# The last four k tiles of the last 512 output features computed token-major in three token groups, in a hybrid decoder step on one core

## The chip, the core and the metric

The kernel runs on one core of a Trainium2 chip. The number that counts is the device time of one execution in microseconds. Before the change it is 1300.18 us, the median of three runs (1300.1 to 1300.28). The engines are named as in the profile: PE multiplies matrices, DVE, ACT and POOL work on tiles, SP issues DMAs. [...] Each engine works through its own queue in order and waits there for what an instruction needs from others.

## What is computed

One layer of a hybrid decoder over 264 tokens (256 of a prompt and 8 samples) and 2048 features. Mixers, gates and projections come first. The change lies in the last two lines of this cut:

```python
def rms_norm(x, g):
    y = x * lax.rsqrt(jnp.mean(x * x, axis=-1, keepdims=True) + EPS)
    return y * g
...
    x = x + (g_a * y_pool + g_b * y_lru + g_c * y_conf) @ w_out
    hid = jnp.square(jax.nn.relu(rms_norm(x, g_mlp) @ w_up))     # 2048 -> 8192
    x = x + hid @ w_down                                         # 8192 -> 2048
...
    y = rms_norm(x, g_final)
```

## The kernel before

**Layout.** Everything is feature-major: a tile has 128 features on the partitions and the 264 tokens (`N`) along the row. The residual `X` is 16 such tiles (`KD`). A product takes a 128x128 piece of a weight matrix as its stationary operand and streams the 264 tokens past it, so a PSUM bank collects one output tile of 128 features by 264 tokens.

**Precision.** Weights arrive as fp32 in `raw`, six slots of 128x1024 filled by DMAs from SP (`dma_pair`, L134). For each such chunk ACT rounds the weights to `whi` (L163) and DVE forms the remainder `wlo` (L164). Activations are kept as such pairs as well; for the last quarter of the MLP they are `LH` and `Q`. Each product is therefore three matmuls (`mm3`, L186 to L188): high by high, high weight by low activation, low weight by high activation.

**Order.** `weight_plan` lists groups of weights; a group is a set of k tiles against 512 output features (four PSUM banks), a chunk is two k tiles of it. The main loop goes through the chunks: it splits the chunk three ahead, sends for the one eight ahead, multiplies the present one, and at the end of a group evacuates the four banks. The MLP is done in four quarters `q`; each quarter computes 2048 hidden features and then multiplies them by 2048 rows of `w_down` in four groups `m` of 512 output features. The very last two chunks are taken together, one output tile after the other, so that the four banks of the last group become complete one at a time.

**The end.** In quarter 3, `down_evac` (L826) adds each finished bank to `X` on DVE. ACT squares the tile into `G` (`square_add`, L795), POOL adds the square to a running sum `sq2` (L798), and ACT scales `X` by the final gain (L837). After the last tile, six matmuls with `ones` (L982) sum the squares over the partitions and spread the sum over all 128 partitions, in two halves of 132 tokens. ACT takes the inverse root (L988), DVE refines it by a Newton step (L994 to L998), and DVE and POOL multiply the 16 tiles of `X` by this factor in pieces (L1003), each piece sent to `y_dram` by a DMA from SP or ACT (L1005). All code after the loop is written out by hand in the order in which each engine gets it.

Of the kernel before, what the change touches and what calls it, by code (L numbers as in the profile page):

```python
# [13 lines left out]
ALU = mybir.AluOpType  # L14
# [7 lines left out]
KD = D // P  # L22
EPS = 1e-6
LN_EXP = "natural_log_exp_and_others"
ROOT = "abs_reciprocal_sqrt_and_small"
# [5 lines left out]
           ("b_lru_x", 8), ("lru_lambda", 8), ("w_conf_conv", 124), ("b_conf_conv", 4), ("g_conf", 4),  # L31
           ("b_conf", 4), ("b_gate", 48), ("g_mlp", 16), ("g_final", 16), ("count", 16)]
PCOL, _at = {}, 0
# [19 lines left out]
SINGLE = 4  # L53
WIDE = 4
ROW = N + CH


def weight_plan():

    groups = [("w_lru_in", 0, 2 * WIDE, 0)] + [("w_in", WIDE, KD - WIDE, m) for m in (1, 2)]
    groups += [("w_in", 0, 16, m) for m in (0, 3, 4, 6, 5)]
    for g in range(4):
        groups += [("w_gate", 0, 16, t) for t in ((0, 4, 1), (5,), (2, 6), (3, 7))[g]]
        groups += [("w_pool_br", 0, 4, g), ("w_lru_br", 0, 8, g)]
    groups += [("w_gate", 0, 16, 8 + g) for g in range(3)]
    groups += [("w_conf_br", 0, 4, 0), ("w_gate", 0, 16, 11)]
    groups += [("w_conf_br", 0, 4, g) for g in range(1, 4)]
    groups += [("w_out", 0, 16, m) for m in range(4)]  # L70
    for q in range(4):
        groups += [("w_up", 0, 16, q * 4 + m) for m in range(4)]
        groups += [("w_down", q * 16, 16, m) for m in range(4)]
    chunks = []
    for gi, (name, _, k, m) in enumerate(groups):
        for c in range(k // 2):
            chunks.append(("wide" if name == "w_lru_in" else "dense", gi, c, CH))
            if name == "w_in" and (m, c) in LRU_AT:
                chunks.append(("lru", LRU_AT.index((m, c)), 0, 512))
            if (name, m) == ("w_gate", 0) and c == 3:  # L80
                chunks += [("grp", 0, 0, 512), ("none", 0, 0, 0)]
    return groups, chunks


@with_exitstack
def hybrid_step(ctx: ExitStack, tc: tile.TileContext, head_in, x_in, par_in, st_in, wall, y_out, st_out):
    nc = tc.nc
# [27 lines left out]
    sp = cpool.tile([P, 16], F32, name="sp")  # L115
    gfin = cpool.tile([P, KD], F32, name="gfin")

# [705 lines left out]
    def half(h):  # L823
        return slice(h * (N // 2), (h + 1) * (N // 2))

    def down_evac(q, m, ps):  # L826
        if (q, m) == (3, KD - 1):
            for h in range(2):
                nc.vector.tensor_tensor(X[:, m, half(h)], X[:, m, half(h)], res(ps)[:, h, :], op=ALU.add)
                nc.vector.tensor_tensor(G[:, 11, half(h)], X[:, m, half(h)], X[:, m, half(h)], op=ALU.mult)  # L830
            return
        nc.vector.tensor_tensor(halves(X[:, m, :]), halves(X[:, m, :]), res(ps), op=ALU.add)  # L832
        spend(dve=0.4)
        if q == 3:
            def rest():
                square_add(m, m < KD - 2)
                nc.scalar.activation(X[:, m, :], X[:, m, :], AF.Copy, scale=gfin[:, m:m + 1])  # L837

            later(0 if m >= KD - 4 else 1 + m % 4 // 2, rest)

# [77 lines left out]
    for i, ch in enumerate(chunks):  # L918
# [18 lines left out]
        if kind == "dense":  # L937
            rhs, fn = group(gi)
            n = groups[gi][2] // 2
            if c == 0:  # L940
                pss = [acc() for _ in range(4)] if gi > 2 else pair[4 * gi - 4:4 * gi]
            if i < len(chunks) - 2:
                for kt in range(2):
                    if i == 13 and kt == 1:
                        x_rms()
                    for m in range(4):
                        tile_mm(i, gi, c, kt, m, rhs, pss, c == n - 1 and kt == 1)
            elif i == len(chunks) - 1:
                for m in range(4):
                    for b in range(4):  # L950
                        tile_mm(i - 1 + b // 2, gi, c - 1 + b // 2, b % 2, m, rhs, pss, b == 3)
            if c == n - 1:
                for m in range(4):
                    fn(m, pss[m])
                after(gi)
        elif kind == "lru":
            for j in range(2):
                lru_gate_mm(2 * gi + j, i, j)
            if gi == 3:
                lru_tail()  # L960
        elif kind == "grp":
            grp_mm(i)
        if i == len(chunks) - 4:
            nc.scalar.preload_act_table_set(ROOT)
        if i == 140:
            nc.sync.dma_start(st_out, st)
        if 5 <= i < 9:
            x_squares(i - 5)
# [9 lines left out]

    ps = [acc(), acc()]
    for k, t in enumerate((20, 21 + (KD - 2) % 3, 11)):  # L980
        for h in range(2):
            nc.tensor.matmul(ps[h][:, half(h)], ones, G[:, t, half(h)], start=k == 0, stop=k == 2)  # L982
    Y = raw.rearrange("p a c -> p (a c)")[:, :KD * N].rearrange("p (h k n) -> p h k n", h=2, k=KD)
    t, last = G[:, 9, :], acc()
    factor, seed2 = G[:, 10, :], G[:, 12, half(1)]

    for h in range(2):
        nc.scalar.activation(rstd[:, half(h)], ps[h][:, half(h)], AF.Abs_reciprocal_sqrt, bias=eps)  # L988
    nc.scalar.activation(X[:, KD - 1, :], X[:, KD - 1, :], AF.Copy, scale=gfin[:, KD - 1:KD])

    def newton(h):
        c = half(h)
        if h:
            nc.vector.scalar_tensor_tensor(t[:, c], ps[h][:, c], EPS, seed2, op0=ALU.add, op1=ALU.mult)  # L994
        else:
            nc.vector.scalar_tensor_tensor(t[:, c], ps[h][:, c], EPS, rstd[:, c], op0=ALU.add, op1=ALU.mult)
            nc.vector.tensor_tensor(t[:, c], t[:, c], rstd[:, c], op=ALU.mult)
        nc.vector.scalar_tensor_tensor(factor[:, c], t[:, c], -3.0, rstd[:, c], op0=ALU.add, op1=ALU.mult)  # L998
        nc.scalar.copy(last[:, c], factor[:, c])

    def scaled(eng, queue, h, a, b, by):
        k = slice(a, b)
        eng.tensor_tensor(Y[:, h, k, :], X[:, k, half(h)], by[:, None, half(h)].to_broadcast([P, b - a, N // 2]),  # L1003
                          op=ALU.mult)
        queue.dma_start(y_out[:, h, k, :], Y[:, h, k, :])  # L1005

    def own(h, a, b):
        scaled(nc.gpsimd, nc.scalar, h, a, b, factor)

    def wide(h, a, b, by=last):  # L1010
        scaled(nc.vector, nc.sync, h, a, b, by)

    newton(0)
    nc.scalar.activation(seed2, rstd[:, half(1)], AF.Square)
    wide(0, 0, 2, factor)
    own(0, 11, 13)
    wide(0, 2, 5)
    wide(0, 5, 8)
    own(0, 13, 16)
    wide(0, 8, 11)  # L1020
    newton(1)
    wide(1, 0, 4, factor)
    own(1, 11, 16)
    wide(1, 4, 11)

# [91 lines left out]
```

## Time and profile before

| | us |
|---|---|
| median of three runs (lowest, highest) | 1300.18 (1300.1, 1300.28) |
| the profiled execution | 1299.8 |
| its span, from first to last instruction | 1298.0 |
| PE busy | 1287.7 |
| DVE busy | 833.2 |
| ACT busy | 718.4 |
| POOL busy | 113.6 |
| mean DMA rate | 198 GB/s |

The profile is one execution. Its span is 1.8 us shorter than that execution's own time, and the execution is 0.4 us faster than the median of the runs. A row of a timeline shows start, duration, engine, line, operation and tiles. `PEld` is the loading of a stationary operand, `SPq` and `ACTq` are the queues that issue DMAs. A mean duration in a group of instructions is that of one instruction, which can be longer than the distance between two, since instructions overlap on an engine.

### The profile page before, as it was taken

What the parts mean: (1) busy time and instruction counts of PE and PEld (TensorE: products, weight loads), DVE (VectorE), ACT (ScalarE), POOL (GpSimd) and SP (SyncE); (2) the same over time, 40 slices, a digit from 0 to 9 for tenths busy, and PEclk for the clock granted to TensorE, in tenths of its full rate; (3) what the DMA queues carried; (4) which work ended last, traced back from release to release, by engine and by line L of the source; (5) the groups of instructions that cost most, each with busy time, mean ns of one, the idle gap of its engine ahead of it and who ended that gap; (6) DMA issues with size and microseconds to landing.
All of it is one profiled execution on the core that took longest, in us unless ns stands there. A gap on an engine that the chain in (4) does not pass through costs nothing.

```text
span 1298.0 us, 26711 instructions
## 1 busy us (share of the span) xinstructions
PE 1287.7 (99%) x11434; PEld 1286.8 (99%) x11434; DVE 833.2 (64%) x1056; ACT 718.4 (55%) x1024; POOL 113.6 (9%) x149
## 2 busy tenths in 40 slices
PE   9999999999999999999999999999999999999997
PEld 9999999999999999999999999999999999999996
DVE  6886898776776677666655455655555655565554
ACT  7767677667674655455544334543344533354544
POOL 0250010110102023131000000000000000000113
PEclk9999999999999999999999999999999999999998
DMA  9655556555565564655555555555555555555561
GB/s 348 214 185 199 196 202 205 194 195 195 199 228 193 185 208 157 233 187 203 196 198 194 196 197 195 195 198 195 196 196 196 194 197 195 196 196 197 196 202 68
DMA packets 39287, 256.96 MB, mean 198 GB/s; under 512 B 4352, under 2 KB 5504, under 8 KB 10240
## 3 DMA queue, kind: packets, MB, share of 16 engines
q1 hardware_dynamic: 38736, 254.58, 57.7%
q8 instruction: 89, 1.46, 0.4%
q10 hardware_dynamic: 432, 0.68, 0.1%
q14 instruction: 30, 0.25, 0.1%
HBM read 252.03 MB, written 3.21 MB: 197 GB/s over the span
## 4 chain that ended last, share of the span: by engine, by line
PE 99%; issue 0%; POOLq 0%; POOL 0%; DVE 0%; ACT 0%; ACTq 0%
PE acc L188 33%; PE acc L186 33%; PE acc L187 33%; PE acc L896 1%; PE acc L302 0%; POOLq L1096 0%; POOL raw L1003 0%; POOL G L798 0%; PE acc L260 0%; DVE X L832 0%; ACT G L795 0%; POOLq L1003 0%; POOLq L798 0%; ACTq L795 0%
## 5 line engine op out<-in xcount | busy, mean ns | idle before, releaser
L164 DVE TENSOR_TENSOR wlo<-raw,whi 128x1024 fp32r<-128x1024 f32 (+1 forms) x479 | 586.4, 1226 | 442.6 <-ACT whi L163 436.8
L163 ACT CAST whi<-raw 128x1024 fp32r<-128x1024 f32 (+1 forms) x479 | 493.4, 1033 | 525.7 <-PE acc L187 478.3
L188 PE MATMUL acc<-A,wlo 128*128 128x264 f32 x1952 | 538.8, 276 | 0.0
L187 PE MATMUL acc<-A,whi 128*128 128x264 f32 x1952 | 538.8, 276 | 0.0
L186 PE MATMUL acc<-A,whi 128*128 128x264 f32 x1952 | 538.7, 276 | 0.0
L186 PEld LDWEIGHTS acc<-A,whi 128*128 128x128 f32 x1952 | 368.9, 189 | 0.0
L187 PEld LDWEIGHTS acc<-A,whi 128*128 128x128 f32 x1952 | 368.9, 189 | 0.0
L188 PEld LDWEIGHTS acc<-A,wlo 128*128 128x128 f32 x1952 | 368.9, 189 | 0.0
L186 PE MATMUL acc<-xn,whi 128*128 128x264 f32 x1024 | 282.6, 276 | 0.0
L187 PE MATMUL acc<-xn,whi 128*128 128x264 f32 x1024 | 282.6, 276 | 0.0
L188 PE MATMUL acc<-xn,wlo 128*128 128x264 f32 x1024 | 282.6, 276 | 0.0
L186 PEld LDWEIGHTS acc<-xn,whi 128*128 128x128 f32 x1024 | 193.5, 189 | 0.0
L187 PEld LDWEIGHTS acc<-xn,whi 128*128 128x128 f32 x1024 | 193.5, 189 | 0.0
L188 PEld LDWEIGHTS acc<-xn,wlo 128*128 128x128 f32 x1024 | 193.5, 189 | 0.0
L187 PE MATMUL acc<-Q,whi 128*128 128x264 f32 x644 | 177.7, 276 | 0.0
L186 PE MATMUL acc<-LH,whi 128*128 128x264 f32 x640 | 176.6, 276 | 0.0
L188 PE MATMUL acc<-LH,wlo 128*128 128x264 f32 x640 | 176.6, 276 | 0.0
L187 PEld LDWEIGHTS acc<-Q,whi 128*128 128x128 f32 x644 | 121.7, 189 | 0.0
L186 PEld LDWEIGHTS acc<-LH,whi 128*128 128x128 f32 x640 | 121.0, 189 | 0.0
L188 PEld LDWEIGHTS acc<-LH,wlo 128*128 128x128 f32 x640 | 121.0, 189 | 0.0
L798 POOL TENSOR_TENSOR G<-G 128x132 f32<-128x132 f32 x56 | 34.3, 641 | 736.7 <-ACT G L795 736.7
L577 ACT ACTIVATE G<-tmp,par 128x256 f32<-128x256 f32 x120 | 54.2, 498 | 2.9 <-DVE G L580 2.1
(188 smaller groups left out, 796.0 us busy)
## 6 DMA issues: line engine op xcount, KB each, us to landing
raw<-wall_dram SPq DMA_DIRECT2D x226, 1024.0 KB, 4.9
raw<-wall_dram SPq DMA_DIRECT2D x18, 512.0 KB, 4.1
raw<-wall_dram SPq DMA_DIRECT2D x5, 256.0 KB, 3.1
X<-x_dram SPq DMA_DIRECT2D x4, 264.0 KB, 8.3
so_dram<-st SPq DMA_DIRECT2D x1, 1018.0 KB, 9.4
st<-st_dram SPq DMA_DIRECT2D x1, 912.0 KB, 10.9
y_dram<-raw SPq DMA_DIRECT2D x3, 198.0 KB, 2.4
X<-x_dram SPq DMA_DIRECT2D x1, 528.0 KB, 9.5
```

The lines of the kernel that those rows point to most:

```text
L163: nc.scalar.copy(h[:, s], r)
L164: nc.vector.tensor_tensor(lo[:, s], r, f(h[:, s]), op=ALU.subtract)
L186: nc.tensor.matmul(ps[:, :N], whi_t, xh, start=first, stop=False)
L187: nc.tensor.matmul(ps[:, :N], whi_t, xl, start=False, stop=False)
L188: nc.tensor.matmul(ps[:, :N], wlo_t, xh, start=False, stop=last)
L577: nc.scalar.activation(dst[:, ct, :TP], vext[:, ct, k:k + TP], AF.Copy, scale=par[:, w:w + 1])
L798: nc.gpsimd.tensor_tensor(sq2[:, half(h)], sq2[:, half(h)], t[:, half(h)], op=ALU.add)
L896: nc.tensor.matmul(pair[m][:, :N], w[:, m * P:(m + 1) * P], sent(A[:, x, :]), start=start and k == 0, stop=False)
```

## The change

Of the last quarter, the fourth group of 512 output features (tiles 12 to 15 of `X`) is moved. Its first twelve k tiles are multiplied before the other three groups. Its last four k tiles (`TAIL`) stay at the very end, but there the tokens are stationary and the 512 features stream: the tokens are cut into three groups of 128, 96 and 40 (`CUT`), and each group takes two halves of 256 features, 12 matmuls each.

```diff
-        groups += [("w_down", q * 16, 16, m) for m in range(4)]
+        groups += [("w_down", q * 16, 16, m) for m in range(4)] if q < 3 else (
+            [("w_down", 48, 16 - TAIL, 3)] + [("w_down", 48, 16, m) for m in range(3)] + [("w_down", KF - TAIL, TAIL, 3)])
```

So that the token-major products can be added to it, the sum of residual and the first twelve k tiles (`held`) is turned token-major during the main loop: DVE transposes 32x32 blocks into `turned`, and 36 DMAs from SP put the blocks in place in `resid`, two at each of 18 chunks.

```diff
     def down_evac(q, m, ps):
-        if (q, m) == (3, KD - 1):
...
+        if q == 3 and m >= KA:
+            nc.vector.tensor_tensor(halves(T["held"][:, m - KA, :N]), halves(X[:, m, :]), res(ps), op=ALU.add)
+            spend(dve=0.4)
+            later(1 + (m - KA) // 2, lambda: turn(m - KA))
             return
...
+    def dma_turned(n):
...
+        nc.sync.dma_start(T["resid"][a:a + r, g, :].rearrange("t (m q f) -> t m q f", m=4, q=4)[:, :, q, :],
+                          T["turned"][32 * q:32 * q + r, :, 32 * j:32 * j + 32])
...
+        if len(chunks) - 23 <= i < len(chunks) - 5:
+            for n in range(2):
+                dma_turned(2 * (i - len(chunks) + 23) + n)
```

The end after the loop is new. For a token group `g`, `half_sum` adds a half to `resid` on DVE, squares it on ACT with the row's sum as a second output, and multiplies it by the final gain on POOL. `close` computes the inverse root per token, which is now one number per partition. The gain of the 512 features is loaded as a row on all partitions. `token_out` scales the rows on ACT and stores them from ACT's queue in a second output, `t_dram`; `spread_mm` turns the factors into a row on all partitions, and `piece` multiplies the twelve feature-major tiles by it and stores them.

```diff
+    def token_mm(g, ps, a, b, steps):
+        for s in steps:
+            kt, way = divmod(s, 3)
...
+            nc.tensor.matmul(ps[:size[g], :b - a], x[:, toks(g)], sent(w), start=s == 0, stop=s == 3 * TAIL - 1)
...
+    def others():
+        for g in range(3):
+            nc.tensor.matmul(inv[:size[g], g:g + 1], sq2[:, toks(g)], ones[:, 0:1], start=True, stop=True)
+
+    def spread_mm(g):
+        fb.append(acc())
+        nc.tensor.matmul(fb[g][:, :size[g]], T["unit"][:size[g], :], diag[g], start=True, stop=True)
...
+    def root(g):
+        n, y = size[g], st_col(3, g)
+        nc.vector.scalar_tensor_tensor(st_col(5, g), st_col(4, g), y, y, op0=ALU.mult, op1=ALU.mult)
+        nc.vector.scalar_tensor_tensor(st_col(6, g), st_col(5, g), -3.0, y, op0=ALU.add, op1=ALU.mult)
+        diag.append(Gf[:n, 4 * N + P * g:4 * N + P * g + n])
+        nc.vector.tensor_scalar(diag[g], T["eye"][:n, :n], st_col(6, g), None, op0=ALU.mult)
...
+    def half_sum(g, h):
+        token_sum(g, bank[g][h], 256 * h, 256 * h + 256)
+        token_square(g, 256 * h, 256 * h + 256, 1 + 6 * h)
+        weighed(g, 256 * h, 256 * h + 256)
+
+    def close(g):
+        seed(g, 7, 2)
+        mean(g, 7, 2, 4)
+        root(g)
+
+    half_mm(0, 0)
+    half_mm(0, 1)
+    half_mm(1, 0, every[:3])
+    others()
+    half_mm(1, 0, every[3:])
+    half_mm(1, 1, every[:5])
+    half_sum(0, 0)
+    half_sum(0, 1)
+    for g in range(3):
+        other_in(g)
+    mean(0, 1, 0, 2)
+    close(0)
+    spread_mm(0)
+    half_mm(1, 1, every[5:])
+    half_sum(1, 0)
+    mean(1, 1, 0, 2)
+    token_out(0)
+    factor_copy(0)
+    piece(0, 0, 3)
+    piece(0, 3, 6)
+    piece(0, 10, 12, True)
+    half_sum(1, 1)
+    piece(0, 6, 10)
+    bank.append([acc(), acc()])
+    half_mm(2, 0)
+    close(1)
+    half_sum(2, 0)
+    mean(2, 1, 0, 2)
+    token_out(1)
+    half_mm(2, 1, every[:6])
+    spread_mm(1)
+    half_mm(2, 1, every[6:])
+    piece(1, 0, 4)
+    half_sum(2, 1)
+    piece(1, 4, 8)
+    close(2)
+    spread_mm(2)
+    token_out(2)
+    piece(1, 8, 12)
+    piece(2, 0, 6)
+    piece(2, 6, 12)
```

What this puts on the engines is shown at three places. Line numbers of the changed program differ from those before. Before, DVE's queue at the end of the program reads (`acc` is a PSUM bank, `raw` is where outputs are put):

```order
L832 TENSOR_TENSOR X<-X,acc 128x264 x3
L829 TENSOR_TENSOR X<-X,acc 128x132
L830 TENSOR_TENSOR G<-X 128x132
L829 TENSOR_TENSOR X<-X,acc 128x132
L830 TENSOR_TENSOR G<-X 128x132
L996 SCALAR_TENSOR_TENSOR G<-acc,rstd 128x132
L997 TENSOR_TENSOR G<-G,rstd 128x132
L998 SCALAR_TENSOR_TENSOR G<-G,rstd 128x132
L1003 TENSOR_TENSOR raw<-X,G 128x264
L1003 TENSOR_TENSOR raw<-X,acc 128x396 x3
```

It closes the norm once for the first half of the tokens and then multiplies. In the changed program, this is DVE's queue from the sums of token group 1 on (`end_13333` holds the one-column statistics, `end_13334` is `resid`, `end_13335` the token-major sum):

```order
L1057 TENSOR_TENSOR end_13335<-end_13334,acc 96x256
L1071 TENSOR_SCALAR end_13333<-end_13333 96x1
L1094 TENSOR_TENSOR raw<-X,acc 128x384 x2
L1057 TENSOR_TENSOR end_13335<-end_13334,acc 96x256
L1094 TENSOR_TENSOR raw<-X,acc 128x512
L1071 TENSOR_SCALAR end_13333<-end_13333 96x1
L1075 SCALAR_TENSOR_TENSOR end_13333<-end_13333 96x1
L1076 SCALAR_TENSOR_TENSOR end_13333<-end_13333 96x1
L1078 TENSOR_SCALAR G<-end_13332,end_13333 96x96
```

The pieces of group 0 (L1094) now stand between the sums and the statistics of group 1, and the same pattern follows for group 2. PE's queue in the changed program at the place where the factors of group 1 are spread (`end_13332` holds the constant ones) is:

```order
L1039 MATMUL acc<-wlo,LH 40x256
L1047 MATMUL acc<-G,end_13332 128x96
L1039 MATMUL acc<-whi,LH 40x256
L1039 MATMUL acc<-whi,Q 40x256
L1039 MATMUL acc<-wlo,LH 40x256
```

The spreading matmul (L1047) stands ahead of the last six products of group 2, which wait behind it. On SP, the end of the weight stream and the first stores read in the changed program:

```order
L152 DMA raw<-wall_dram 128x1024 x2
L856 DMA end_13334<-end_13333 32x4x32 x6
L856 DMA end_13334<-end_13333 8x4x32 x4
L1097 DMA y_dram<-raw 128x384 x2
L1097 DMA y_dram<-raw 128x256
L1097 DMA y_dram<-raw 128x512
```

The last ten of the 36 placing DMAs (L856) come after the last weights, and the third store (128x256), which POOL makes, stands ahead of the fourth.

## What the change was predicted to do

> **What bounds the kernel now.** I began with the page: the busy times and the chain that ended last.
>
> ```profile
> span 1298.0 us, 26711 instructions
> PE 1287.7 (99%) x11434; PEld 1286.8 (99%) x11434; DVE 833.2 (64%) x1056; ACT 718.4 (55%) x1024; POOL 113.6 (9%) x149
> PE 99%; issue 0%; POOLq 0%; POOL 0%; DVE 0%; ACT 0%; ACTq 0%
> ```
>
> PE carries the whole kernel up to its last product, and only what comes after that can be hidden. So the second view is the timeline of the end, engine by engine; first PE.
>
> ```profile
> 1283.46 0.28 PE L188 MATMUL acc<-LH,wlo 128*128 128x264 f32 x1
> ...
> 1286.50 0.28 PE L188 MATMUL acc<-LH,wlo 128*128 128x264 f32 x1
> 1286.61 1.90 PE L982 MATMUL acc<-G,ones 128*128 128x132 f32 x12
> ```
>
> Between the first two rows lie 27 products, so one takes 3.04/27 = 0.1126 us. The next one could start at 1286.61, and the last is complete at 1286.78. From there to 1298.0 the tail takes 11.2 us. DVE in that time:
>
> ```profile
> 1286.81 0.29 DVE L829 TENSOR_TENSOR X<-X,acc 128x132 f32<-128x132 f32 x1 [0.92 <-PE acc L188]
> ...
> 1289.08 0.29 DVE L998 SCALAR_TENSOR_TENSOR G<-G,rstd 128x132 f32<-128x132 f32 x1
> ...
> 1289.76 1.51 DVE L1003 TENSOR_TENSOR raw<-X,acc 128x396 f32<-128x396 f32 x3
> ...
> 1292.46 1.11 DVE L1003 TENSOR_TENSOR raw<-X,acc 128x924 f32<-128x924 f32 x1
> ```
>
> The norm takes it until 1289.4, the multiplications until 1293.57. The stores, and the time from issue to landing:
>
> ```profile
> 1291.88 2.10 POOL L1003 TENSOR_TENSOR raw<-X,G 128x660 f32<-128x660 f32 x1 [0.45 <-DVE G L998]
> 1294.02 0.34 ACTq L1005 DMA_DIRECT2D y_dram<-raw  x1
> ...
> y_dram<-raw ACTq DMA_DIRECT2D x1, 330.0 KB, 3.0
> y_dram<-raw SPq DMA_DIRECT2D x1, 132.0 KB, 1.8
> y_dram<-raw ACTq DMA_DIRECT2D x1, 132.0 KB, 2.2
> ```
>
> POOL's last piece ends at 1293.98, its store lands at 1294.02 + 3.0 = 1297.0, and 1.0 us of closing follows. The change can only win if this 11.2 us shrinks by more than PE's work grows.
>
> **What it does to PE.** Removed are 4 tiles x 4 k tiles x 3 = 48 products, 48 x 0.1126 = 5.40 us, and the six matmuls of L982. The loop thus ends 5.40 us earlier, at 1281.21. Added are 3 groups x 2 halves x 12 = 72 products of 256 columns. Scaled by columns one takes 0.1126 x 256/264 = 0.109, all 7.86 us; not scaled, 8.11. I take the first, because the rows are back to back with nothing between. [...]
>
> That is the weak side of the change: 264 tokens cost three passes over the features where one did it before, +2.46 us. The fp32 matmuls (three for `others`, three spreads) replace the six of L982: 1.90/6 is at most 0.32 each; with one column or fewer tokens I take 0.5 for `others` and 0.23 for a spread, between nothing and 0.32 each.
>
> **Small operations.** The new code lives on one-column steps. Nearest rows:
>
> ```profile
> L182 DVE TENSOR_TENSOR st<-acc,rstd 128x8 f32<-128x8 f32 x8 | 1.3, 157 | 0.0
> L693 DVE SCALAR_TENSOR_TENSOR G<-G,st 128x8 f32<-128x8 f32 x4 | 0.7, 172 | 0.1
> L348 DVE TENSOR_SCALAR G<-par 128x8 f32<-128x8 f32 x1 | 0.1, 119 | 0.0
> L252 DVE TENSOR_SCALAR G<-G 128x264 f32<-128x264 f32 x3 | 0.9, 297 | 0.1
> L832 DVE TENSOR_TENSOR X<-X,acc 128x264 f32<-128x264 f32 x63 | 22.9, 421 | 6.4 <-PE acc L188 6.4
> L795 ACT ACTIVATE G<-X 128x264 f32<-128x264 f32 x31 | 12.7, 411 | 5.8 <-DVE X L832 5.8
> L344 ACT ACTIVATE G<-par 128x8 f32<-128x8 f32 x1 | 0.2, 205 | 0.0
> 1288.02 0.37 ACT L988 ACTIVATE rstd<-acc,eps 128x132 f32<-128x132 f32 x1 [1.06 <-PE acc L982]
> 1288.42 0.29 DVE L996 SCALAR_TENSOR_TENSOR G<-acc,rstd 128x132 f32<-128x132 f32 x1 [0.46 <-ACT rstd L988]
> ```
>
> A mean or an added epsilon takes 0.16 (0.11 until the next can start), a Newton step 0.17, the 128x128 diagonal 0.20 (between L348 and L252), each with 0.04 after the step it needs. A sum of 256 takes 0.41, a square 0.41, with 0.09 from DVE to ACT and 0.03 back (1288.39 to 1288.42). The seed lies between L344's 0.205 and L988's 0.37; I take 0.26. A square that also gives its sum is not in the trace: between the plain 0.41 and 0.41 + 0.205 for another tiny ACT step; I take 0.41, the row it is nearest to. A piece goes by L1003: 1.51/3 = 0.50 for 396, and (1.11 - 0.56)/528 = 1.05 ns per element, so 384 take 0.50, 512 take 0.62, 240 take 0.34.
>
> **The new tail, along DVE's queue.**
>
> ```profile
> 1284.11 0.43 DVE L832 TENSOR_TENSOR X<-X,acc 128x264 f32<-128x264 f32 x1 [0.92 <-PE acc L188]
> 1285.20 0.89 POOL L798 TENSOR_TENSOR G<-G 128x132 f32<-128x132 f32 x2 [0.46 <-ACT G L795]
> ```
>
> The tile evacuated from 1284.11 had its square added by POOL at 1286.09, 1.98 later. In the new order the last tile is evacuated 5.40 us before 1286.81, at 1281.41, so the sum `sq2` that `others` needs is there at 1283.4.
>
> Group 0: its second half is complete at 1281.21 + 24 x 0.109 + 0.17 = 1284.00. The sum ends at 1284.44, the square at 1284.95. Meanwhile PE has done three more products and `others` (1284.85). Three epsilons and a mean end at 1285.36, the seed at 1285.71, two Newton steps and the diagonal at 1286.40.
>
> Group 1: sum, square and the way back to DVE, 0.41 + 0.09 + 0.41 + 0.03: 1287.30. DVE stands there for 0.5 us, because the mean that wants this square is queued ahead of the pieces of group 0, whose stores wait with it. Mean 0.11 and two pieces of 384: 1288.41. Second sum 0.36: 1288.77; its square and seed (until 1289.62) run beside the piece of 512. Newton steps and diagonal 0.62: 1290.27.
>
> Group 2: sum, square and back: 1291.21. Mean and one piece: 1291.82. Second sum 0.41: 1292.22; its square, until 1292.72, beside a piece of 0.50. Seed 0.30, then 0.65 to the end of the diagonal: 1293.67. Last piece of group 1: 1294.17, under it the spread. Two pieces of 240: 1294.93. The last store (120 KB) by the two 132 KB rows, 1.8 and 2.2: 2.1 with its issue, 1297.07. With closing 1.0: **1298.1**.
>
> PE waits for this chain and not the reverse: at the spread of group 1, until 1290.35, from 1289.40, with six products behind it. They are complete at 1291.45, when DVE is still busy. So the tail after the last product shrinks from 11.2 to 6.6 us, but that product comes 4.7 us later: 2.46 of products, 1.2 of fp32 matmuls that were in the tail before, and about 1.0 of waiting.
>
> ACT and POOL lie beside it. POOL multiplies six halves by the gain:
>
> ```profile
> L749 POOL TENSOR_TENSOR tmp<-G 128x264 f32<-128x264 f32 x8 | 9.7, 1244 | 122.5 <-DVE G L746 122.5
> L752 POOL TENSOR_TENSOR G<-G,tmp 128x264 f32<-128x264 f32 x16 | 14.2, 921 | 43.0 <-DVE G L746 43.0
> L837 ACT ACTIVATE X<-X,gfin 128x264 f32<-128x264 f32 x15 | 7.7, 516 | 0.5
> ```
>
> At 0.9 each the last is done at 1293.2, ahead of the scale factor (1293.43). The scaling of 512 columns on ACT takes at most two of L837, until 1294.5, and its store lands by 1296.7. At L749's 1.24 the last product on POOL ends at 1293.5, still no later than the chain. The third store on SP waits for POOL's own piece until 1289.8 and holds the fourth by 0.7 us, which is over long before the end.
>
> **The main loop.** Four transposes of 128x288 are not in the trace: between 0.30 (L252) and twice L832. DVE idles 1.48 us in a chunk there (row of 1274.28), so nothing either way. The 36 DMAs stand in SP's queue between the weights.
>
> ```profile
> 1243.13 19.23 SPq L146 DMA_DIRECT2D raw<-wall_dram  x8
> ...
> raw<-wall_dram SPq DMA_DIRECT2D x226, 1024.0 KB, 4.9
> raw<-wall_dram SPq DMA_DIRECT2D x18, 512.0 KB, 4.1
> ...
> 1274.28 1.22 DVE L164 TENSOR_TENSOR wlo<-raw,whi 128x1024 fp32r<-128x1024 f32 x1 [1.48 <-ACT whi L163]
> ...
> 1275.90 1.04 ACT L163 CAST whi<-raw 128x1024 fp32r<-128x1024 f32 x1 [1.65 <-PE acc L187]
> ```
>
> The last weights are sent for at about 1262.0, land 4.1 later and are used at 1275.90: 9.8 us to spare. Two small DMAs per chunk, 0.34 us of issue each as in ACTq's row, cost nothing under that cover; without it, each us of delay would be a us of PE. How long runs of 128 bytes take from SBUF to SBUF, no row shows. [...]
>
> **Sum.** Span 1298.1 against 1298.0: +0.1 on the profiled 1299.8. The median of the runs is 0.4 above that execution: 1300.3. This is no change within 0.2% (2.6 us, about what a measurement of this kernel can tell).
>
> Ends of the unknown: one-column steps, 13 on the chain, from 0.119 to 0.297, -0.6 to +1.6; squares with sums, four on the chain, 0 to +0.8; seeds 0.205 to 0.37, -0.2 to +0.3; `others` 0 to 0.96, -0.3 to +0.5; landing 1.8 to 2.2, -0.3 to +0.1. Together -1.4 to +3.3: 1298.9 to 1303.6.
>
> **Rivals.**
> *Better cover.* If DVE didn't stand for the first squares of groups 1 and 2 (0.5 each) and the steps were at their low ends (-1.4), 1297.9 comes out. For it: ACT is otherwise nearly idle. Against: DVE's order is fixed, and the mean precedes the pieces.
> *Dear small steps (slower).* In `close` and `mean`, on DVE and ACT, 17 steps hang on one another across engines. At 0.30 each (L252, L998, hardly less for many fewer columns) and 0.2 for each summed square, plus the fp32 end, +3.0: 1303.3. It decides from +0.15 per step. For it: L996 to L998 cost 0.33 each for 132 columns. Against: L182, L693.
> *Weights late (slower).* If the small DMAs held weights back by over 9.8 us, PE would stand; a delay of twice that gives 1300.3 + 9.8 = 1310. [...]
> *Not what it says.* If the norm chain, and not the products, paces all three groups, the products hide nothing more. That is largely my forecast, already paid with 1.0 of PE's wait.
>
> **Chances.** Forecast 0.62, better cover 0.16 (a third of it under 1297.6), dear steps 0.18 (four fifths over 1302.9), weights late 0.04. So faster 0.05, slower 0.18, same 0.77. The range leaves out a tenth on each side: 1298.2 to 1303.6.
>
> **What would show it.** The loop's last tile evacuated at about 1281.4, and weights never waited for, show the shift right. DVE standing 0.5 us for ACT twice, and PE standing about 1 us at the second spread, show the chain. The last product at about 1291.4 and the last store's issue at 1294.9 show the sum. I am wrong if one-column steps take over 0.25, if the summed square exceeds 0.5, if 256-column products don't come every 0.109 us, or if ACT waits for `raw`.

## The result, and the profile after

The changed kernel takes 1302.13 us (median of 22 runs, 1301.47 to 1302.56), the kernel before in the same sessions 1300.05 us (22 runs, 1299.57 to 1300.51). The ratio is 1.0016, with a 95% interval of 1.0009 to 1.0022: 2.1 us slower, just inside the 0.2% that the prediction called no change. Forecast was +0.1 us on the span of the profiled execution, measured is +2.1 (1298.0 to 1300.1). So 2 us of cost appeared somewhere that the sum didn't hold, and the runs below look for them.

The page of the changed kernel begins:

```profile
span 1300.1 us, 26856 instructions
PE 1290.4 (99%) x11458; PEld 1289.3 (99%) x11458; DVE 838.4 (64%) x1078; ACT 720.8 (55%) x1032; POOL 112.0 (9%) x152
PE 98%; DMA 0%; DVE 0%; ACT 0%; issue 0%; DVEq 0%; ACTq 0%; SPq 0%
```

Busy times say nothing here: the whole difference lies in the last 20 us. The timeline of DVE (start, duration, engine, line, operation, and in brackets the idle time ahead and what ended it) shows where:

```profile
1281.42 0.43 DVE L838 TENSOR_TENSOR X<-X,acc 128x264 f32<-128x264 f32 x1 [0.92 <-PE acc L194]
1284.10 0.42 DVE L1057 TENSOR_TENSOR end<-end,acc 128x256 f32<-128x256 f32 x1 [0.92 <-PE acc L1039]
...
1286.32 0.29 DVE L1078 TENSOR_SCALAR G<-end,end 128x128 f32<-128x128 f32 x1
1286.64 0.42 DVE L1057 TENSOR_TENSOR end<-end,acc 96x256 f32<-96x256 f32 x1
1287.64 0.21 DVE L1071 TENSOR_SCALAR end<-end 96x1 f32<-96x1 f32 x1 [0.58 <-ACT G L1061]
1288.99 1.02 DVE L1094 TENSOR_TENSOR raw<-X,acc 128x384 f32<-128x384 f32 x2 [1.14 <-ACT end L1087]
...
1291.68 0.27 DVE L1078 TENSOR_SCALAR G<-end,end 96x96 f32<-96x96 f32 x1
1292.08 0.41 DVE L1057 TENSOR_TENSOR end<-end,acc 40x256 f32<-40x256 f32 x1
...
1295.41 0.24 DVE L1078 TENSOR_SCALAR G<-end,end 40x40 f32<-40x40 f32 x1
1295.56 0.54 DVE L1094 TENSOR_TENSOR raw<-X,acc 128x384 f32<-128x384 f32 x1
1296.45 0.72 DVE L1094 TENSOR_TENSOR raw<-X,acc 128x240 f32<-128x240 f32 x2 [0.34 <-PE acc L1047]
```

The loop's last tile is evacuated at 1281.42, forecast 1281.41: the shift of 5.40 us is there. The diagonal of group 0 is complete at 1286.61, forecast 1286.40. Then the forecast is left behind: the first piece starts at 1288.99, not at 1287.41, after an idle time of 1.14 that a copy on ACT (L1087) ends. From the end of group 0's diagonal to the end of DVE's last piece (1297.17) the trace has 10.56 us, the forecast had 1294.93 - 1286.40 = 8.53. This stretch, 2.03 too long, is the yardstick below; it doesn't depend on when the loop ends, which differs between the profiled executions of all kernels below by up to 0.6 us (that tile is evacuated at 1281.42 to 1282.03).

What ACT did meanwhile:

```profile
1287.10 0.42 ACT L1061 ACTIVATE G<-end 96x256 f32<-96x256 f32 x1 [1.35 <-DVE end L1057]
1287.42 0.19 ACT L1061 ACTIVATION_READ_ACCUMULATOR G<-end 96x1 f32 x1
1287.52 0.71 ACT L1083 ACTIVATE raw<-first,end 128x512 f32<-128x512 f32 x1
1288.25 0.39 ACTq L1084 DMA_DIRECT2D t_dram<-raw  x1
1288.69 0.27 ACT L1087 COPY end<-acc 128x128 f32<-128x128 f32 x1 [0.46 <-ACT raw L1083]
```

Each square with a sum brings a row of its own for reading the sum, 0.19 long and ending 0.09 to 0.10 after the square. Then come the scaling of group 0's 512 columns (`token_out`), the issue of its store, and only then the copy of group 0's factors from PSUM (`factor_copy`), which POOL reads for its own piece. DVE's pieces don't read that copy; they read the bank. Yet they stand behind it.

PE, at the two later spreads (the bracket is PE's idle time ahead of them):

```profile
1292.09 0.43 PE L1047 MATMUL acc<-G,end 96*128 96x96 f32 x2 [2.15 <-DVE G L1078]
...
1295.79 0.62 PE L1047 MATMUL acc<-G,end 40*128 40x40 f32 x2 [2.61 <-DVE G L1078]
```

PE waits for DVE, 2.15 us at group 1 where 1.0 was forecast, and again 2.61 at group 2, where the forecast's times leave about 2.2 (products complete at 1291.45, the diagonal at 1293.67). The products are not what is late.

### The profile page after: what moved, and what is told of

It is laid out like the page before. It is cut to its first block, busy times and chain, and to the rows that moved or that the text cites. A ratio compares the mean times of both kernels' runs of the same rounds, so it can differ in the third digit from the quotient of the medians.

```text
span 1300.1 us, 26856 instructions
## 1 busy us (share of the span) xinstructions
PE 1290.4 (99%) x11458; PEld 1289.3 (99%) x11458; DVE 838.4 (64%) x1078; ACT 720.8 (55%) x1032; POOL 112.0 (9%) x152
## 4 chain that ended last, share of the span: by engine, by line
PE 98%; DMA 0%; DVE 0%; ACT 0%; issue 0%; DVEq 0%; ACTq 0%; SPq 0%
PE acc L192 32%; PE acc L194 32%; PE acc L193 32%; PE acc L933 1%; DMA first<-head_dram 0%; PE acc L1039 0%; DMA y_dram<-raw 0%; DVE raw L1094 0%; DVE end L1057 0%; ACT G L1061 0%; PE acc L1047 0%; ACT raw L1083 0%; ACT end L1068 0%; PE acc L266 0%; PE acc L1043 0%
## 5 line engine op out<-in xcount | busy, mean ns | idle before, releaser
L193 PE MATMUL acc<-Q,whi 128*128 128x264 f32 x628 | 173.3, 276 | 0.0
L192 PE MATMUL acc<-LH,whi 128*128 128x264 f32 x624 | 172.2, 276 | 0.0
L194 PE MATMUL acc<-LH,wlo 128*128 128x264 f32 x624 | 172.2, 276 | 0.0
L193 PEld LDWEIGHTS acc<-Q,whi 128*128 128x128 f32 x628 | 118.7, 189 | 0.0
L192 PEld LDWEIGHTS acc<-LH,whi 128*128 128x128 f32 x624 | 117.9, 189 | 0.0
L194 PEld LDWEIGHTS acc<-LH,wlo 128*128 128x128 f32 x624 | 117.9, 189 | 0.0
```

Source lines behind the costliest of these rows:

```text
L192: nc.tensor.matmul(ps[:, :N], whi_t, xh, start=first, stop=False)
L193: nc.tensor.matmul(ps[:, :N], whi_t, xl, start=False, stop=False)
L194: nc.tensor.matmul(ps[:, :N], wlo_t, xh, start=False, stop=last)
```

## The experiments

Each kernel was timed beside the kernel before. The stretch is that of the profiled execution, from the end of group 0's diagonal to the end of DVE's last piece; the median span is over all executions of the kernel.

| kernel | median us | ratio to before (95%) | median span | stretch |
|---|---|---|---|---|
| after | 1302.13 | 1.0016 (1.0009 to 1.0022) | 1300.4 | 10.56 |
| copy ahead | 1300.98 | 1.0007 (0.9997 to 1.0016) | 1299.3 | 9.37 |
| means later | 1302.42 | 1.0019 (1.001 to 1.0028) | 1300.7 | 10.64 |
| fewer products | 1302.24 | 1.0016 (1.0007 to 1.0025) | 1300.5 | 10.55 |
| no placing DMAs | 1302.47 | 1.0017 (1.0008 to 1.0026) | 1300.4 | 10.20 |
| copy ahead, no sums | 1300.67 | 1.0004 (0.9995 to 1.0013) | 1299.0 | 9.01 |
| copy ahead, idle products | 1301.28 | 1.001 (1.0001 to 1.0019) | 1299.4 | 9.06 |
| sums first | 1301.48 | 1.0011 (1.0002 to 1.002) | 1299.4 | 8.96 |
| order | 1300.31 | 1.0001 (0.9992 to 1.001) | 1298.6 | 8.99 |
| order, one operand | 1300.12 | 1.0 (0.9991 to 1.0009) | 1298.4 | 8.61 |
| order, no copy | 1300.12 | 1.0 (0.9991 to 1.0009) | 1298.3 | 8.54 |
| order, no copy, idle products | 1300.26 | 1.0001 (0.9992 to 1.001) | 1298.1 | 8.25 |

The kernel before took 1300.11, 1300.21 and 1300.16 us in the three sessions of the experiments.

### The copy ahead of the scaling

```diff
-    token_out(0)
     factor_copy(0)
+    token_out(0)
     piece(0, 0, 3)
```

> Only the order on ACT changes: the copy of group 0's factors stands ahead of the scaling of group 0's token rows and of its store, instead of behind them. Theory A (the miss of 2 us is mostly DVE's first piece of group 0 waiting for that copy, 1.14 us in the changed kernel's trace, because both read the same PSUM bank and the program orders them): DVE's idle time ahead of that piece falls from 1.14 us to under 0.2, everything behind it on DVE moves up, and the time falls by 0.9 to 1.1 us, from 2.1 above the kernel before to about 1.0 above it. Theory B (the end is paced by the products and the one-column steps, the copy has slack): no change, 2.1 above.

DVE and ACT in this kernel:

```profile
1288.06 0.21 DVE L1071 TENSOR_SCALAR end<-end 96x1 f32<-96x1 f32 x1 [0.58 <-ACT G L1061]
1288.20 1.02 DVE L1094 TENSOR_TENSOR raw<-X,acc 128x384 f32<-128x384 f32 x2
...
1287.93 0.24 ACT L1087 COPY end<-acc 128x128 f32<-128x128 f32 x1
1288.08 0.73 ACT L1083 ACTIVATE raw<-first,end 128x512 f32<-128x512 f32 x1
```

The idle time of 1.14 is gone, the pieces follow the mean at once, the stretch is 1.19 shorter and the median 1.15. The one swapped pair of lines accounts for more than half of the excess.

Why does an instruction on DVE wait for a copy on ACT that it doesn't use? Both read the same tile in the same bank of PSUM, and in these runs the two reads keep the order in which the code has them. In "sums first", where a piece is written ahead of the copy, it is the copy that waits for the piece:

```profile
1288.13 0.27 ACT L1087 COPY end<-acc 128x128 f32<-128x128 f32 x1 [0.22 <-DVE raw L1094]
```

No run here takes the order away, and none has the two engines read different tiles of a bank, so neither what keeps the order, nor what would happen without it, nor whether it goes by bank or by tile is shown.

### The means later in DVE's queue

```diff
     half_sum(1, 0)
-    mean(1, 1, 0, 2)
...
     piece(0, 10, 12, True)
+    mean(1, 1, 0, 2)
     half_sum(1, 1)
...
     half_sum(2, 0)
-    mean(2, 1, 0, 2)
...
     piece(1, 0, 4)
+    mean(2, 1, 0, 2)
     half_sum(2, 1)
```

> Only DVE's order changes: the first mean of group 1 goes behind two pieces of group 0, that of group 2 behind one piece of group 1, so that DVE does not stand for ACT's squares (0.58 us twice in the changed kernel). Theory A: at group 1 nothing is gained, since the pieces wait for the copy anyway (0 to +0.1); at group 2 the piece starts 0.6 earlier but the next sum then waits for PE's last products, 0.45 gained: together -0.3 to -0.5 us. Theory B (dear one-column steps decide, their place does not): 0. Better cover, the rival of the prediction, would have it at -1.0.

A miss: no gain. DVE's rows say why. (Here `token_out(0)` still stands ahead of the copy.)

```profile
1289.45 1.02 DVE L1094 TENSOR_TENSOR raw<-X,acc 128x384 f32<-128x384 f32 x2 [1.93 <-ACT end L1087]
...
1295.19 0.20 DVE L1071 TENSOR_SCALAR end<-end 40x1 f32<-40x1 f32 x1 [0.51 <-ACT G L1061]
```

In group 0 the 0.58 that DVE no longer spends on the mean it spends on the copy: 1.93 instead of 0.58 and 1.14 with a mean between them. In group 2 the piece does fill the first wait, but ACT is then in `token_out(1)` and its store, and squares the second half 0.41 later; the wait returns in front of the last mean. A stand is worth nothing if what ends the next one hasn't moved.

### Fewer products

```diff
     def half_mm(g, h, steps=every):
+        if g == 2:
+            steps = [s for s in steps if s in (0, 11)]
         token_mm(g, bank[g][h], 256 * h, 256 * h + 256, steps)
```

> Leaves out 20 of the 24 token-major products of token group 2 (2.2 us of PE by 0.111 us each), so the last 512 features of the last 40 tokens lack them. Theory A (DVE's queue paces the end from group 1 on, PE waits for it): at most 0.5 us less, because only the last sum of group 2 waits for PE at all. Rival (the three passes over the features are what the change costs): 2.2 us less, level with the kernel before.

Twenty products, 2.2 us of PE's time, are gone and nothing changes: the stretch is 10.55, and PE only stands longer at the spread of group 1:

```profile
1292.29 0.71 PE L1047 MATMUL acc<-G,end 96*128 96x96 f32 x2 [3.78 <-DVE G L1078]
```

So behind group 1 the products cost nothing, and the chain of norm steps on DVE and ACT sets the pace.

### Without the placing DMAs

```diff
         nc.gpsimd.memset(T["unit"], 1.0)
+        nc.gpsimd.memset(T["resid"], 0.0)
...
-        if len(chunks) - 23 <= i < len(chunks) - 5:
-            for n in range(2):
-                dma_turned(2 * (i - len(chunks) + 23) + n)
```

> The kernel after, without the 36 DMAs that bring the transposed features to their token rows (the rows are zero instead, so the last 512 features lack the residual and the first twelve k tiles). Theory: they lie between weight loads with several us to spare, and cost nothing: 1302.1, within 0.3 of the kernel after, and the loop's last tile is evacuated at the same time. Rival: they hold up the weights or the sums of the groups, and the time falls by 0.5 or more.

The time doesn't fall, as the theory said; weights were never late. One detail speaks for the rival without paying. These are DVE's diagonals of groups 0 and 1 and the sums behind them that read `resid`, in this kernel:

```profile
1286.77 0.28 DVE L1076 TENSOR_SCALAR G<-end,end 128x128 f32<-128x128 f32 x1
1286.97 0.41 DVE L1055 TENSOR_TENSOR end<-end,acc 96x256 f32<-96x256 f32 x1
...
1292.00 0.27 DVE L1076 TENSOR_SCALAR G<-end,end 96x96 f32<-96x96 f32 x1
1292.18 0.41 DVE L1055 TENSOR_TENSOR end<-end,acc 40x256 f32<-40x256 f32 x1
```

The sums start 0.20 and 0.18 after the start of the diagonals. In the kernel after it is 0.32 and 0.40 (rows above), with short waits of 0.05 each in DVE's queue between. The stretch is 0.36 shorter in the profiled execution, the median span is the same 1300.4, and the median time is 0.3 above that of the kernel after. The 0.36 came back behind DVE's last piece: from its end to the end of the span this execution takes 3.25 us, the kernel after 2.93. Why that is longer here isn't shown.

### Squares without their sums

```diff
     def st_col(k, g):
+        if k in (1, 7):
+            return Gf[:size[g], 256 * (k // 7):256 * (k // 7) + 1]
         return stat[:size[g], k, g:g + 1]
...
-        nc.scalar.activation(Gf[:size[g], a:b], V[:size[g], g, a:b], AF.Square, accum_out=st_col(k, g))
+        nc.scalar.activation(Gf[:size[g], a:b], V[:size[g], g, a:b], AF.Square)
```

> The kernel with the copy ahead of the scaling, its squares without the sum that ACT gathers beside them: the mean reads the square of one feature in the sum's place (so all scale factors are others), and it waits for the same instructions as before. Theory: the extra row of 0.19 us behind each square ends 0.10 later than the square alone, and about four of the six stand on the chain: 0.4 to 0.7 faster than the first experiment, 1300.3 to 1300.6. Rival: reading the sum is hidden in the way from ACT to DVE: within 0.15 of 1301.0.

0.31 faster than "copy ahead" in the median, 0.36 in the stretch: the reading of the sums costs some 0.09 at each of four places on the chain, a little less than expected. The intervals of the two ratios overlap, so it is the traces that carry this. DVE's wait for the first square of group 1 shows one of them:

```profile
1287.99 0.21 DVE L1073 TENSOR_SCALAR end<-G,end 96x1 f32<-96x1 f32 x1 [0.49 <-ACT G L1063]
```

It was 0.58 with the sum.

### Other orders

"Sums first" moves the second sums and the first piece ahead, gives POOL larger pieces (3 and 4 tiles, the latter behind a second copy) and puts group 0's scaling behind group 1's norm. Its core:

```diff
     half_sum(1, 0)
-    mean(1, 1, 0, 2)
-    token_out(0)
-    factor_copy(0)
     piece(0, 0, 3)
...
+    factor_copy(0)
+    mean(1, 1, 0, 2)
     half_sum(1, 1)
...
+    piece(0, 9, 12, True)
...
+    factor_copy(1)
...
+    piece(1, 8, 12, True)
```

> The same operations in another order: on DVE each group's sums and statistics go ahead of pieces, which fill the waits; the copies of the factors go ahead of the row scalings on ACT; all products of group 2 ahead of the second spread; and POOL makes 384 elements of group 0 and 384 of group 1 instead of 256 of group 0. Theory A (the order of waits on DVE and ACT is what costs, the work itself fits): DVE's last piece ends 2.5 to 3 us earlier, at about 1294.2 of the span instead of 1297.2, and the time falls to 0 to 1 us below the kernel before. Theory B (products and one-column steps): no better than 1.5 us above the kernel before.

A miss: 0.65 below the kernel after, not below the one before. Two rows of it, DVE's and POOL's:

```profile
1289.63 0.88 DVE L1075 SCALAR_TENSOR_TENSOR end<-end 96x1 f32<-96x1 f32 x1
...
1289.50 1.00 POOL L1094 TENSOR_TENSOR raw<-X,end 128x384 f32<-128x384 f32 x1
```

A Newton step of one column, 0.22 elsewhere, takes 0.88 and ends at 1290.51, together with POOL's piece (1290.50). That is not all of the miss: the stretch, 8.96, is as short as that of "order" below (8.99), but from the last piece to the end of the span this kernel takes 3.44 us and "order" 2.79, and its diagonal of group 0 comes 0.33 later behind the loop's last tile.

"Order" starts from "copy ahead" and is meant to avoid all stands seen so far:

```diff
-    half_mm(1, 0, every[:3])
     others()
-    half_mm(1, 0, every[3:])
+    half_mm(1, 0)
...
     half_sum(1, 0)
-    mean(1, 1, 0, 2)
-    factor_copy(0)
     token_out(0)
     piece(0, 0, 3)
+    mean(1, 1, 0, 2)
     piece(0, 3, 6)
+    factor_copy(0)
...
-    close(1)
+    half_mm(2, 1)
+    seed(1, 7, 2)
     half_sum(2, 0)
-    mean(2, 1, 0, 2)
-    token_out(1)
...
+    mean(1, 7, 2, 4)
+    root(1)
     spread_mm(1)
...
+    token_out(1, nc.sync)
+    mean(2, 1, 0, 2)
     half_sum(2, 1)
+    piece(1, 0, 4)
```

> The tail's instructions in another order, none left out: `others` right behind group 0's products, the scaling and its store of group 0 ahead, the means of groups 1 and 2 behind work that doesn't wait, the first sum of group 2 ahead of group 1's diagonal, group 1's scaled rows stored by SP's queue. Theory: what is left of the excess is DVE standing for ACT and for PE, about 2.1 us between the diagonal of group 0 and the end in the first experiment; the order takes some 1.2 us of it away and 0.3 ahead of that diagonal: 1299.5, below the kernel before. Rival: the idle time only moves to other waits, as it did when the means alone were moved: 1301 or more.

1300.31: equal to the kernel before within the interval, but 0.67 below "copy ahead" where 1.5 was expected. Two things eat the rest, a new wait for the copy, and again a Newton step beside POOL:

```profile
1289.20 0.69 DVE L1094 TENSOR_TENSOR raw<-X,acc 128x512 f32<-128x512 f32 x1 [0.37 <-ACT end L1087]
...
1290.71 0.65 DVE L1076 SCALAR_TENSOR_TENSOR end<-end 96x1 f32<-96x1 f32 x1
...
1289.94 1.40 POOL L1065 TENSOR_TENSOR first<-end,end 96x256 f32<-96x256 f32 x2
```

0.65 where 0.16 is usual, and it ends at 1291.36 with POOL's multiplication (1291.34).

### One operand, and no copy

```diff
-        nc.vector.scalar_tensor_tensor(st_col(5, g), st_col(4, g), y, y, op0=ALU.mult, op1=ALU.mult)
-        nc.vector.scalar_tensor_tensor(st_col(6, g), st_col(5, g), -3.0, y, op0=ALU.add, op1=ALU.mult)
+        nc.vector.tensor_scalar(st_col(5, g), st_col(4, g), y, y, op0=ALU.mult, op1=ALU.mult)
+        nc.vector.tensor_scalar(st_col(6, g), st_col(5, g), -3.0, y, op0=ALU.add, op1=ALU.mult)
```

> The reordered tail, with both Newton steps written as tensor_scalar with the seed as a scalar, so that each reads one tensor of SBUF where it read two. Theory: in the reordered kernel the second Newton step of group 1 took 0.65 us where 0.15 is usual, and ended together with POOL's multiplication by the gain, because a DVE instruction with two SBUF operands waits for POOL's to end; with one operand it takes 0.15 beside POOL, and the kernel 0.5 less: 1299.8. Rival: a one-column step is slow beside POOL whatever its operands, or the time is lost elsewhere: 1300.3, and the long step is there again.

```profile
1291.01 0.21 DVE L1076 TENSOR_SCALAR end<-end 96x1 f32<-96x1 f32 x1
1291.26 0.42 DVE L1078 TENSOR_SCALAR G<-end,end 96x96 f32<-96x96 f32 x1
...
1290.20 1.40 POOL L1065 TENSOR_TENSOR first<-end,end 96x256 f32<-96x256 f32 x2
```

Beside the same work of POOL the step takes 0.21 with one tensor operand, so it was the form with two. The gain is less than expected: the steps are 0.05 longer in this form, and the diagonal behind them now takes 0.42 (0.27 elsewhere). From the diagonal of group 0 to that of group 1 it takes 4.69 us instead of 4.94, which is 0.25. The stretch falls by 0.38, but 0.23 of that lies behind the last diagonal and isn't the operands' doing: the last spread takes 0.38 us here and 0.62 in "order" (more on this under the idle products). In the profiled execution 0.31 comes back after the last piece (3.10 us to the end, 2.79 in "order"), and the medians differ by 0.19, less than can be told. The two long steps end with POOL's instruction, within 0.02 us (1290.51 and 1290.50, 1291.36 and 1291.34); why they wait for it isn't shown. In the kernel after, no Newton step runs beside POOL, so none of its 2 us is of this kind.

The next kernel takes the copy and POOL's piece out of the last one as well:

```diff
     piece(0, 3, 6)
-    factor_copy(0)
-    piece(0, 10, 12, True)
     half_sum(1, 1)
-    piece(0, 6, 10)
+    piece(0, 6, 9)
...
     spread_mm(1)
+    piece(0, 9, 12)
```

> The same, and the copy of group 0's factors and POOL's own piece are gone: DVE multiplies twelve tiles of group 0 in four pieces, the last behind group 1's diagonal. Theory: the 0.36 us more of DVE's work are less than the wait for the copy and stand beside the spread of group 1; the diagonal of group 1 is complete 1.0 to 1.2 earlier than in the reordered kernel, and the time is 1299.0 to 1299.4. Rival: DVE is then busy throughout and its own work (or the landing of stores that stand closer together) sets the end: 1299.8 or more.

A miss: the same 1300.12, with two tiles more on DVE and none on POOL. The diagonal of group 1 is complete 4.18 us after that of group 0, where it was 4.94 in "order" and 4.69 with one operand: 0.76 earlier than in "order", not 1.0 to 1.2. At the end little is left of it (8.54 against 8.61). Part of the reason is the rival's: between 1288 and 1294 DVE is busy for 5.50 of 6 us, and the diagonal of group 2 comes 7.03 us after that of group 0, with one operand 7.32. The rest is the last spread, which takes 0.61 here, with DVE waiting 0.34 for it, and 0.38 with one operand. The windows of this kernel (start and end, length, busy time of PE, PEld, DVE, ACT and POOL with counts, granted clock, DMA share, GB/s):

```profile
1288.00:1290.00 2.00, 2.00 (x21) 2.00 (x19) 1.86 (x7) 1.26 (x5) 0.83 (x2) 1.00 0.57 212
1290.00:1292.00 2.00, 1.25 (x10) 0.85 (x8) 1.82 (x8) 1.27 (x4) 0.73 (x2) 1.00 0.58 214
1292.00:1294.00 2.00, 0.00 (x0) 0.03 (x1) 1.82 (x7) 1.07 (x4) 0.72 (x1) 0.85 0.83 282
```

POOL's share of the pieces, with the copy that it reads, had been worth nothing that can be told.

### Idle products to keep the clock

While PE stood for the last diagonal (2.61 us in the kernel after), its granted clock fell, from 1.00 (1294 to 1295) to 0.51 (1295 to 1296). The same view of "copy ahead", and of that kernel with 20 products that nobody reads in front of the last spread:

```profile
1294.00:1296.00 2.00, 0.62 (x2) 0.50 (x2) 1.47 (x7) 0.89 (x2) 0.08 (x1) 0.61 0.81 270
```

```profile
1294.00:1296.00 2.00, 1.02 (x8) 0.64 (x6) 1.76 (x7) 0.91 (x2) 0.12 (x1) 1.00 0.82 272
```

```diff
     close(2)
+    warm = acc()
+    for s in range(20):
+        token_into(warm, s)
     spread_mm(2)
```

> The kernel with the copy ahead of the scaling (first experiment), plus 20 products of 256 columns that nobody reads, on PE between group 2's last product and the spread of group 2. Theory: that spread took 0.62 us because the granted clock had fallen to 0.5 after 2.6 us without work; with PE at work it takes about 0.43, the last two pieces start 0.2 earlier and the kernel takes 1300.8. Rival: the clock isn't the cause of the 0.62, or the products hold the spread up: no change, 1301.0, or up to 0.3 slower.

The gain isn't there. The idle products do keep the clock, the spread takes 0.41 instead of 0.62, and DVE's last pieces no longer wait for it:

```profile
1294.95 0.41 PE L1051 MATMUL acc<-G,end 40*128 40x40 f32 x2 [0.34 <-DVE G L1082]
...
1294.81 1.30 DVE L1098 TENSOR_TENSOR raw<-X,acc 128x384 f32<-128x384 f32 x3
```

The stretch is 0.31 shorter, the median span 0.1 longer. From the end of the last piece to the end of the span it is now 1299.4 - 1296.11 = 3.29 us, before 1299.3 - 1296.39 = 2.91. So the 0.3 was given back after the last piece. The stores show how: SP's last issue ends at 1296.91 in "copy ahead" and at 1296.68 here, but the last two stores, of 120 KB each, take 2.0 us from issue to landing there and 2.3 here (medians). The three last stores follow closer on one another here; that this is what makes them slower is the likely reading and not a trial.

The pattern holds over nearly all versions. Where the last spread took about 0.4 and DVE's last three pieces followed at once (the two kernels with idle products, "sums first", "one operand"), 3.10 to 3.44 us pass from the last piece to the end of the span. Where DVE waited 0.34 for a spread of 0.62, it is 2.79 to 2.99, except without the placing DMAs (3.25).

The length of PE's stand alone doesn't decide whether the clock falls. In "sums first" PE stood longer, without idle products, and its last spread took 0.38, not 0.62:

```profile
1294.71 0.38 PE L1047 MATMUL acc<-G,end 40*128 40x40 f32 x2 [3.13 <-DVE G L1078]
```

In "one operand" the spread took 0.38 as well, after 2.20 us, and the clock from 1294 to 1296 was 0.95; in "order" it was down to 0.50 in the same 2 us, after a stand of 2.10. What decides the moment isn't shown.

The same products on top of "order, no copy":

> The same, and 20 products that nobody reads on PE behind group 2's last one (2.2 us), so that the granted clock doesn't fall before the spread of group 2. Theory: that spread takes 0.43 in place of 0.62, and what came back in the earlier trial with such products was the stores' landing, 0.3 later because they stood closer: here the stores start earlier, so 0.2 is kept, 1298.9 to 1299.2. Rival: the landing of the stores sets the end: the same as without them, or 0.1 to 0.3 slower; the spread may also stand behind the products, since the diagonal comes earlier here.

Median span 1298.1 instead of 1298.3, median time 0.14 higher: no difference that can be told. The stretch fell by 0.29 and the rest of the span grew from 2.83 to 3.14; the last two stores take 2.2 us from issue to landing instead of 1.9. No version tried is faster than the kernel before.

## Why the prediction was right or wrong

**The main loop** was right. The shift by 5.40 us came out; that it did so to 0.01 is luck, since the same point lies up to 0.6 us later in the other executions. The 36 small DMAs cost no time that can be measured, and the rival "weights late" fell: without the DMAs the time is the same. The four transposes were not taken out by themselves; no time of theirs shows at the loop's end. The DMAs take 4.1 us to land, and the last weights 5.8 instead of 4.1 (3.7 without the DMAs; all are medians), 1.7 of the margin of 9.8.

```profile
end<-end SPq DMA_DIRECT2D x32, 16.0 KB, 4.1
raw<-wall_dram SPq DMA_DIRECT2D x18, 512.0 KB, 5.8
```

**The products** were right: 256 columns come every 0.109 us with 96 and 40 tokens, and every 0.112 with 128 (24 of them from 1281.22 to 1283.90).

**The verdict** was right, within 0.2%, and the reason "PE waits for this chain and not the reverse" was too: 20 products less change nothing. That is the rival "not what it says" as well, which the prediction had folded into its forecast; the wait at the spread of group 1 is 2.15 us instead of 1.0. That the verdict held with a wait of 1.2 us missing from the sum is owed to the width of the 0.2%, 2.6 us.

**The size** was wrong: +2.1 us on the span against +0.1. The step that failed is "Mean 0.11 and two pieces of 384: 1288.41". It let the pieces of group 0 start as soon as the mean was through, since the spread was done, and held that ACT lies beside the chain. The prediction had reckoned with POOL's piece, and with its store, which holds another back; it had not seen that DVE's pieces read the bank that the copy reads, and that the copy stood on ACT behind a scaling of 0.71 and the issue of a store of 0.39. That is 1.19 us, shown by swapping two lines. It is a wait that the dependencies of the data don't show and the order of the code does.

**The summed squares** were taken at 0.41, the end of the bounds nearest to the plain row. They end 0.09 to 0.10 later, together 0.36 on the four places of the stretch. The forecast said that it would be wrong if a summed square exceeded 0.5; it reached 0.51 to 0.52.

**The other small steps** were about right: means 0.21 for 0.16, Newton steps 0.22 and 0.16 for 0.17, seeds 0.29 for 0.26, diagonals 0.24 to 0.29 for 0.20. "Dear small steps" fell as a rival: what it priced at 0.30 each costs 0.2, and the time went to waits.

**The last spread** was hidden "under" the last piece of group 1 in the forecast. It takes 0.62 at the lowered clock (0.51 from 1295 to 1296) and leaves a wait of 0.34; the trial with idle products shows that this wait can go and the time stays.

**The sum itself** has small slips, none over 0.1 us. By its own terms group 0's diagonal ends at 1286.36 and not 1286.40 (1285.71 + 0.65; the next time, 1287.30, goes on from 1286.36), group 1's steps take 0.65 and not 0.62, and two pieces of 240 at 0.34 end at 1294.85 and not 1294.93.

The account, with the fifth term as what is left over: diagonal of group 0 +0.21, copy +1.19, sums of squares +0.36, waits ahead of the sums that read `resid` +0.36, the rest of the stretch +0.12, the way from the last piece to the end -0.24 (2.93 against 3.17). That is +2.0 on the span, 1300.1 against 1298.1. The fourth term is from one profiled execution, in which 0.32 of it came back behind the last piece, and did not show in the time, so it is no shown cost of the kernel; the first, the fifth and the last ones are differences between two traces and a forecast, not trials.

**Better cover** had the right idea, that DVE's stands could be avoided, and the wrong price. Avoiding most of them took the kernel from 1302.13 to 1300.12, to where it began, not below.

## What to carry to other kernels

When one engine's result in PSUM has two readers, look at what stands ahead of each of them in its queue: here the earlier one in the code held the later one for 1.14 us, though both only read. Moving such a copy ahead of work that nobody waits for cost one line here and gave back 1.15 of 2.1 us. And when a dependent chain of small steps is to be hidden behind products, count the length of the chain first: here it needed 8.3 to 10.6 us behind the first diagonal, against 5.2 us of products (48 of 0.109) for the last two groups, part of them done ahead of it, so the products could not cover it.

## What the runs showed of the hardware

- A square with its sum as a second output on ACT leaves a second row of 0.19 us and ends 0.09 to 0.10 later than the square alone.
- A one-column DVE step with two tensors from SBUF, begun beside a POOL multiplication, lasted until that ended, within 0.02 (0.88 and 0.65 instead of 0.22 and 0.16); with one tensor it took 0.21.
- The granted clock of PE fell from 1.00 to 0.51 within the 2.61 us that it stood, though PE had been busy for 99% of the span; the following spread took 0.62 instead of 0.41. After 2.10 us in "order" it had fallen too (0.50 from 1294 to 1296, spread 0.62), not so after 2.20 in "one operand" (0.95, spread 0.38); after 3.13 in "sums first" the spread took 0.38.
- A gain of 0.3 us on the last computing engine was lost again, in both kernels with idle products, between its last instruction and the end of the span: the last two stores, of 120 KB each, took 2.3 and 2.2 us from issue to landing instead of 2.0 and 1.9.
